# A hybrid attention and RG-LRU block on one Trainium2 core: output-weight passes on GpSimd's DMA queue, a new step order in attention's projection, and another cut of the last rows

## The chip, the cores and the metric

One core of a Trainium2 chip. The metric is the device time of one execution in microseconds. The kernel before took 924.3 us (median of three runs: 921.23, 924.3 and 924.6).

## The reference, cut to what matters

Sequence length and model width are both 1024, everything is float32, and there is one layer.

```python
shift, scale, gate = split(c @ w_ada + b_ada, 3)
h = rmsnorm(x, norm_g) * (1 + scale) + shift
q, k, v, g_attn, xr, g_rnn, m_attn, m_rnn = split(h @ w_in)
y_attn = sliding_window_attention_with_sinks(rope(q), rope(k), v, sinks) * silu(g_attn)
y_rnn = rg_lru(causal_conv4(xr), ...) * silu(g_rnn)
merged = sigmoid(m_attn) * (y_attn @ w_attn_proj) + sigmoid(m_rnn) * (y_rnn @ w_rnn_proj)
x = x + gate * (merged @ w_out)
return rmsnorm(x, final_g)
```

Attention has 16 heads of 64 with 4 key and value heads, blocks of 128 and a window of 128. The three matrix products that the change lies around are `y_rnn @ w_rnn_proj`, `y_attn @ w_attn_proj` and `merged @ w_out`, each 1024 x 1024 x 1024.

## The kernel before, in words

**Precision.** A float32 operand is split into a high part, which ScalarE makes by a cast to fp32r (`cast`, L104, tile `wh` for weights), and a low part, which VectorE makes as the difference (`rest`, L110, tile `wl`). Each product of two operands is three matmuls: high by high, high by low, low by high. So for each half of a weight block (128 x 512) there is a load into a tile `r`, a cast on ScalarE, a subtraction on VectorE, and only then may TensorE use it. Larger products save multiplications in the manner of Strassen: sums and differences of quadrants, seven products in place of eight.

**Order.** Each engine runs its instructions in the order in which the code was written. In the input projection a small planner fills the slots: `run` goes through products of 12 matmuls, a slot of 2.75 us each (`SLOT`, L686), and places background steps from the lists `waiting[0]`, `waiting[1]` and `waiting[2]` where VectorE and ScalarE have room by the planner's own count (`Load.dve`, `Load.act`, `Load.pe`). After the input projection the order is written out by hand. DMAs are issued by SP, and a few by POOL (GpSimd's queue); SP and POOL issue in order, so a DMA whose data isn't there yet holds those behind it in the same queue.

**Stages**, in us of the profiled execution: norm and adaLN to about 113, input projection to about 553, attention's opening to about 620 and the rest of attention to 742, attention's projection to 833, the output product from 833 to the last matmul at about 916.

**Output-weight passes.** `out_weights(kc, cols)` (L1164) prepares `w_out`: eight passes (four row blocks `kc`, two column halves). A pass loads two pieces of `w_out` into the tiles `wq` (`load`, two DMAs of 256 KB), multiplies both by the adaLN gate (`gated`, two VectorE instructions, L1176), and forms sums and differences for the seven products (`one`, `two`, four VectorE instructions of half size, L1181 to L1187). Four stores bring the seven parts to `wq_d` in DRAM. The four tiles are the same for all passes, so a pass's load waits for the stores of the pass before it. The steps stand last in `waiting[2]`, each behind the condition `idle` (L1160); what the input projection doesn't place is left for `outs(n)`, which places `n` steps at a time during attention's projection.

**RNN projection.** It runs as filler inside attention: `rp_steps` yields one `part` per attention unit and calls `load_y` for the next group of `y_rnn` (tiles `yh`, `yl`, from the scratch `yh_d`, `yl_d`, L1441 to L1445).

**Attention's projection** (L1790 to L1840) has eight blocks `c` of 128 output columns, in turn in the PSUM tiles `rp` and `pmain`. After the matmuls of block c are written (`ap_k`), VectorE gets `merge2(c-1)` (projection result times gate, plus the RNN part: two instructions of 128x1024), `naturals(c-1)` (ScalarE cast to `hh`, VectorE rest `hl`: the left operand of the last product), `merge1(c)` (L1726, needs the loads `m`, `smr`), then `prep_r` for the weights of block c+1, then three or four pass steps (`outs`) and for c over 4 the quadrant sums (`sums`). `merge_loads(c+1)` issues the three loads that the merges of block c+1 need.

**The output product** (L1862 on) goes by 24 steps n = 0..23, each 12 x 4 matmuls into four of eight PSUM banks `bo`, and a last round that is done row by row (p = 6). `prep_right(n+4)` splits the weights `wr` four steps ahead. At n = 3 ScalarE copies four banks into the four others (`A.copy(b1[i], b2[i])`, L1929); step n = 4 adds to these copies. From n = 21 on the first half of the final norm's rows is scaled (`row1`, tile `xo`), and the last round ends with `row2` for each of four row blocks: root of the mean square, scale on ScalarE and VectorE, store.

## Time and profile before

| | us |
|---|---|
| median of the runs | 924.3 |
| profiled execution, its own time | 925.58 |
| its span, first instruction to last | 923.9 |
| TensorE busy in the span | 896.8 (97%) |
| VectorE busy | 722.7 (78%) |
| ScalarE busy | 555.7 (60%) |
| GpSimd busy | 90.7 (10%) |

The 1.68 us between the profiled execution's time and its span lie outside the recorded instructions. A row of a timeline gives start, duration, engine, line, operation, output and inputs, the number of merged instructions, and in brackets the idle time ahead of it with what ended that. TensorE's matmuls are pipelined, so a row of one matmul shows 0.39 us although the next starts 0.23 us later.

### The profile page before, as it was taken

The page shows a single profiled execution, that of the slowest core. Times are in us where ns is not written, and L with a number is a line of the kernel's source. Part 1 is how long each engine was busy: PE and PEld are TensorE (multiplying, and loading weights), DVE is VectorE, ACT ScalarE, POOL GpSimd, SP SyncE. Part 2 cuts the span into 40 slices and gives each one's busy share as a digit, 9 for nine tenths or more (in the row PEclk, how much of TensorE's full clock was granted, in tenths as well). Part 3 has the DMA queues.
Part 4 walks back from the last instruction along what each step waited for, and adds up shares of the span by engine and source line. Part 5 has one row for each costly group of instructions (what it writes and reads, how often), then busy time and mean ns, then how long its engine had stood idle before and what let it go on. Part 6 is the DMA issues. An engine that isn't in the chain of part 4 may idle for free.

```text
span 923.9 us, 12581 instructions
## 1 busy us (share of the span) xinstructions
PE 896.8 (97%) x4187; PEld 741.8 (80%) x4187; DVE 722.7 (78%) x1139; ACT 555.7 (60%) x1084; POOL 90.7 (10%) x156
## 2 busy tenths in 40 slices
PE   5999999999999999999999999999999999998996
PEld 4789888887888888888887888888888878776885
DVE  7976889797659975997677776898999738669675
ACT  6753655554557646775596785887878611114554
POOL 0110000000000000000000002544354300000002
PEclk9999999999999999999999999999999999999999
DMA  9943459862342651445145349996665188896214
GB/s 354 414 168 113 166 169 322 276 210 79 115 137 91 205 200 49 148 165 192 57 147 196 102 171 335 350 349 211 196 202 167 57 289 276 306 368 239 66 58 168
DMA packets 97047, 182.06 MB, mean 197 GB/s; under 512 B 13891, under 2 KB 41539, under 8 KB 96982
## 3 DMA queue, kind: packets, MB, share of 16 engines
q1 hardware_dynamic: 93940, 173.11, 54.3%
q0 software_dynamic: 2752, 7.83, 2.4%
q8 instruction: 33, 0.54, 0.2%
q10 hardware_dynamic: 290, 0.32, 0.1%
q14 instruction: 32, 0.26, 0.1%
HBM read 124.49 MB, written 57.12 MB: 197 GB/s over the span
## 4 chain that ended last, share of the span: by engine, by line
PE 74%; DMA 11%; DVE 9%; ACT 3%; issue 2%; SPq 1%; POOL 0%; DVEq 0%; ACTq 0%; POOLq 0%
PE bk L693 43%; PE rp L174 7%; PE bo L1862 5%; PE pgate L988 5%; PE bk L174 3%; PE pv L1350 2%; PE s_ps L1278 2%; DMA wq_d<-wq 2%; PE pmain L174 2%; DMA yl<-yl_d 1%; DMA wq<-w_out 1%; PE pt L1316 1%; DMA r<-w_rp 1%; DVE wl L110 1%; DMA r<-w_main 1%
## 5 line engine op out<-in xcount | busy, mean ns | idle before, releaser
L693 PE MATMUL bk<-nh,wl 128*128 128x512 f32 x352 | 137.6, 391 | 1.4 <-DVE wl L110 1.4
L693 PE MATMUL bk<-nh,wh 128*128 128x512 f32 x352 | 137.3, 390 | 0.0
L693 PE MATMUL bk<-nl,wh 128*128 128x512 f32 x352 | 137.2, 390 | 0.0
L110 DVE TENSOR_TENSOR wl<-r,wh 128x512 fp32r<-128x512 f32 x113 | 80.7, 728 | 19.7 <-ACT wh L104 19.7
L104 ACT CAST wh<-r 128x512 fp32r<-128x512 f32 x113 | 68.6, 618 | 35.2 <-PE bk L1524 12.2
L693 PEld LDWEIGHTS bk<-nh,wl 128*128 128x128 f32 x352 | 66.1, 188 | 16.3 <-DVE wl L110 2.7
L693 PEld LDWEIGHTS bk<-nh,wh 128*128 128x128 f32 x352 | 66.1, 188 | 13.6
L693 PEld LDWEIGHTS bk<-nl,wh 128*128 128x128 f32 x352 | 66.1, 188 | 13.6
L693 PE MATMUL bk<-hh,wh 128*128 128x512 f32 x176 | 68.7, 390 | 0.0
L693 PE MATMUL bk<-hh,wl 128*128 128x512 f32 x176 | 68.6, 390 | 0.0
L693 PE MATMUL bk<-hl,wh 128*128 128x512 f32 x176 | 68.6, 390 | 0.0
L110 DVE TENSOR_TENSOR wl<-ws,wh 128x512 fp32r<-128x512 f32 x76 | 51.7, 684 | 0.5 <-ACT wh L104 0.5
L1302 ACT ACTIVATE p<-p,small 128x129 f32<-128x129 f32 x128 | 50.1, 400 | 0.0
L60 POOL DMA_DIRECT2D yh_d<-yh x1 | 0.6, 557 | 493.8 <-ACT yh L1055 493.8
L104 ACT CAST wh<-ws 128x512 fp32r<-128x512 f32 x76 | 45.8, 613 | 1.2 <-DVE ws L715 1.1
L1862 PE MATMUL bo<-wh,sum 128*128 128x512 f32 x128 | 39.6, 390 | 0.0
L693 PEld LDWEIGHTS bk<-hh,wh 128*128 128x128 f32 x176 | 33.1, 188 | 7.6 <-ACT wh L104 0.9
L693 PEld LDWEIGHTS bk<-hl,wh 128*128 128x128 f32 x176 | 33.1, 188 | 6.9
L693 PEld LDWEIGHTS bk<-hh,wl 128*128 128x128 f32 x176 | 33.1, 188 | 6.7
L1278 PE MATMUL s_ps<-ks,qs 128*128 128x256 f32 (+1 forms) x256 | 37.6, 289 | 0.1
L796 ACT ACTIVATE c<-bk 128x512 f32<-128x512 f32 x29 | 17.3, 597 | 32.8 <-PE bk L693 32.8
L693 PE MATMUL bk<-hha,wl 128*128 128x512 f32 x88 | 34.4, 391 | 0.1
(408 smaller groups left out, 2326.2 us busy)
## 6 DMA issues: line engine op xcount, KB each, us to landing
r<-w_main SPq DMA_DIRECT2D x100, 256.0 KB, 4.3
wada<-w_ss SPq DMA_DIRECT2D x16, 512.5 KB, 8.8
qs<-q_d SPq DMA_DIRECT2D x16, 512.0 KB, 6.6
wq_d<-wq SPq DMA_DIRECT2D x24, 256.0 KB, 6.2
wr<-wq_d SPq DMA_DIRECT2D x24, 256.0 KB, 5.0
ks<-k_d SPq DMA_DIRECT2D x24, 192.0 KB, 4.7
q_d<-rhi SPq DMA_DIRECT2D x16, 256.0 KB, 4.1
q_d<-rlo SPq DMA_DIRECT2D x16, 256.0 KB, 4.2
```

The costliest lines, as they stand in the source:

```text
L60: return eng.dma_start(dst, src)
L104: A.copy(dst[0][:], src)
L110: V.tensor_tensor(out=dst[1][:], in0=src, in1=f32(dst[0][:]), op=ALU.subtract)
L174: mm = T.matmul(ps[hf], ww, xx[kc][hf], start=(kc == 0 and ww is w_h and xx is xh), stop=(kc == KC - 1 and xx is xl))
L693: W["pe"] = T.matmul(ps, ww[:, c], b[kc][xx_], start=(first and kc == 0 and i == 0), stop=(kc == 3 and i == 2), skip_group_check=not first)
L796: A.activation(t["t"], s(), AF.Tanh, scale=0.5)
L988: W["pe"] = T.matmul(ps[:, SL[hf]], ww[:, c0:c0 + P], xx_[:, SL[hf]], start=(ic == 0 and i == 0), stop=(ic == 1 and i == 2))
L1278: W["pe"] = T.matmul(o, qs[:, j, qc], ks[:, b, k0 + (0 if n else P):k0 + 256], start=(b == 0), stop=(b == 1))
L1302: A.activation(px[:, j, :], px[:, j, :], AF.Exp, bias=sm[:, 0, j:j + 1], accum_out=sm[:, 1, j:j + 1])
L1316: W["pe"] = T.transpose(pt[:, j, :], px[:, j, 0:P], ident[:])
L1350: W["pe"] = T.matmul(pv[:], b, m[:].rearrange("p j q -> p (j q)"), start=(i == 0), stop=(i == len(prods) - 1))
L1862: T.matmul(bank[p][i] if dst is None else dst, a[:, ts_], b[:][:, sl], start=(new and kc == 0 and j == 0), stop=(kc == 3 and j == 2), skip ...
```

## The change

Four things change.

1. The six DMAs of an output-weight pass are issued on POOL (argument `G`) in place of SP. The load no longer waits for `idle`. `idle` is false from slot 130 on, and two stretches of slots (`ROOMY`) let a step in although gate steps wait, where the planner's count has VectorE at most 2.8 us ahead of TensorE. With that, three passes and the load of the fourth stand ahead of attention (before: two passes, and the load of the third, whose arithmetic and stores stood at attention's opening). Five passes' arithmetic and four loads are left for attention's projection (before: five and five).
2. `load_y` is called one unit sooner for the last four groups.
3. In attention's projection the weights of block c+1 are prepared ahead of the merges, `merge1(c)` stands ahead of `merge2(c-1)`, `sma` is loaded in a step of its own (`merge_load2`), passes and sums come last, and the first weights of the output product (`load_b11`, `prep_right(0..3)`) and the sums stand one to two blocks away from where they stood. The copies of the PSUM banks stand ahead of `prep_right(7)`. `fg_bc` and all loads of `x1` move to n = 0.
4. Last rows: the first half of `xo` is multiplied by `fg_bc` at n = 9 and 10 (four VectorE instructions of 128x512), so that `row1` scales that half on ScalarE and VectorE does the other half; two rows stand at n = 21 and two at n = 22 (before: one and three). In the last round the matmuls, addition and square of the last row's first cut stand ahead of the root of row 2.

```diff
+    ROOMY = (52, 56), (111, 117)
...
     def idle():
-        return not waiting[0] or waiting[0][0] in asks
+        t = W["slot"]
+        return t < 130 and (not waiting[0] or waiting[0][0] in asks or (
+            any(a <= t < b for a, b in ROOMY) and Load.dve <= Load.pe + 2.8))
...
         def load():
             for t, k in ((t1, kc), (t2, kc + 4)):
                 dma(t[:], w_out[k * P:(k + 1) * P, :].rearrange(
-                    "p (a t) -> p a t", a=2)[:, :, cols])
+                    "p (a t) -> p a t", a=2)[:, :, cols], G)
...
-            dma(wq_d[kc][:, 0, cols], b11)
-            dma(wq_d[kc][:, 3:5, cols], t2[:])
+            dma(wq_d[kc][:, 0, cols], b11, G)
+            dma(wq_d[kc][:, 3:5, cols], t2[:], G)
...
-            dma(wq_d[kc][:, 1:3, cols], t3[:])
+            dma(wq_d[kc][:, 1:3, cols], t3[:], G)
...
-            dma(wq_d[kc][:, 5:7, cols], t4[:])
-
-        return [idle, [("S", 0, 0, load)], slots(2), idle, [("D", 0, 1.38, gated)], idle,
-                [("D", 0, 0.84, one)], idle, [("D", 0, 0.84, two)], slots(2)]
+            dma(wq_d[kc][:, 5:7, cols], t4[:], G)
+
+        return [[("S", 0, 0, load)], slots(2), idle, [("D", 0, 1.38, gated)], idle,
+                [("D", 0, 0.84, one)], idle, [("D", 0, 0.84, two)], slots(1)]
...
         for i, (c, k) in enumerate(seq):
             part(c, k)
-            if i in (1, 2, 3, 4):
-                load_y(i + 3)
+            if i in (0, 1, 2, 3):
+                load_y(i + 4)
...
+
+    def merge_load2(c):
         ss[c] = tpool.tile([P, S], F32, tag="ss", name="sma", bufs=2)
         dma(ss[c][:], sma_d[c])
...
-    merge2(0)
-    naturals(0)
     merge1(1)
     merge_loads(2)
+    merge2(0)
+    merge_load2(2)
+    naturals(0)
     outs(4)
     for c in range(2, KC):
         ps[c] = new_ps()
         ap_k(c, range(KC))
         if c + 2 < KC:
             load_r(KC + c + 2)
-        merge2(c - 1)
-        naturals(c - 1)
+        if c + 1 < KC:
+            for i in range(2):
+                prep_r(KC + c + 1, i)
         merge1(c)
         if c + 1 < KC:
             merge_loads(c + 1)
-            for i in range(2):
-                prep_r(KC + c + 1, i)
-        if c == 4:
-            fg_bc = W["tout"].tile([P, S], F32, tag="rp", name="fg_bc")
-            dma(fg_bc[:], rows[0:1, D:2 * D].to_broadcast([P, D]))
+        merge2(c - 1)
+        if c + 1 < KC:
+            merge_load2(c + 1)
+        naturals(c - 1)
+        if c < 5:
+            outs(4)
+        if c > 5:
+            for n in ((0,), (1, 2, 3))[c - 6]:
+                prep_right(n, first_w[n])
+        if c in (5, 6):
+            sums(c - 5)
         if c == 5:
-            for i in range(2):
-                load_x1(i, "xo", 2)
-        if c == 6:
             load_b11()
-            prep_right(0, first_w[0])
-        if c == 7:
-            for n in (1, 2):
-                prep_right(n, first_w[n])
-        if c < 6:
-            outs(4)
-        if c > 4:
-            sums(c - 5)
-        if c == 7:
-            prep_right(3, first_w[3])
...
     def row1(i):
-        V.scalar_tensor_tensor(out=x1[i][:], in0=x1[i][:], scalar=pcol(0, i), in1=fg_bc[:],
-                               op0=MUL, op1=MUL)
+        a, b = [x1[i][:, t] for t in SL]
+        A.activation(a, a, AF.Copy, scale=pcol(0, i))
+        V.scalar_tensor_tensor(out=b, in0=b, scalar=pcol(0, i), in1=fg_bc[:, SL[1]], op0=MUL,
+                               op1=MUL)
         dma(out[i * P:(i + 1) * P, :], x1[i][:])
...
-    def row2(i, f, eng=nc.sync):
+    def scale2(i, f, eng=nc.sync):
         a, b = x2[i]
-        root(f)
         A.activation(b, b, AF.Copy, scale=f[:, 3:4])
         V.scalar_tensor_tensor(out=a, in0=a, scalar=f[:, 3:4], in1=fg_bc[:, SL[0]], op0=MUL,
                                op1=MUL)
...
         if n == 0:
             naturals(7)
-            for i in range(2):
-                load_x1(2 + i, "ss", 2)
-        if n + 4 < 28:
-            prep_right(n + 4)
-        if n == 2:
-            sums(3)
+            for i in range(4):
+                load_x1(i, "ss" if i > 1 else "xo", 2)
+            fg_bc = W["tout"].tile([P, S], F32, tag="rp", name="fg_bc")
+            dma(fg_bc[:], rows[0:1, D:2 * D].to_broadcast([P, D]))
         if n == 3:
             for i in range(4):
                 A.copy(b1[i], b2[i])
+        if n + 4 < 28:
+            prep_right(n + 4)
+        if n in (2, 4):
+            sums(2 if n == 2 else 3)
...
-        at = {4: ("S1", 0), 5: ("S1", 1), 8: ("NS4", 0), 10: ("NS4", 1), 12: ("S2", 0),
+        at = {5: ("S1", 0), 7: ("S1", 1), 8: ("NS4", 0), 10: ("NS4", 1), 12: ("S2", 0),
               14: ("S2", 1), 16: ("NS3", 0), 18: ("NS3", 1)}
...
+        if n in (9, 10):
+            for i in (2 * n - 18, 2 * n - 17):
+                TT(out=x1[i][:, SL[0]], in0=x1[i][:, SL[0]], in1=fg_bc[:, SL[0]], op=MUL)
         if n == 21:
             roots1()
-            row1(0)
-        if n == 22:
-            for i in range(1, 4):
+        if n in (21, 22):
+            for i in (2 * n - 42, 2 * n - 41):
                 row1(i)
...
+    fs = [small() for _ in range(3)]
+
+    def last_cut(h, f):
+        sl = slice(256 * h, 256 * h + 256)
+        for kc in range(4):
+            products(6, kc, 3, b1[2 + h][:, 0:256], sl, True)
+        add_x(x2[3][0][:, sl], b1[2 + h][:, 0:256], ADD)
+        square(x2[3][0][:, sl], f[:, 1:2] if h else f[:, 4:5], 256)
     for i in range(3):
-        f = small()
+        f = fs[i]
         guard(f, pcol(8, i))
         for kc in range(4):
             products(6, kc, i)
         add_x(x2[i][0], b2[i], ADD)
         square(x2[i][0], f[:, 1:2])
-        row2(i, f)
+        if i < 2:
+            root(f)
+            scale2(i, f)
     f = small()
-    cuts = [slice(0, 256), slice(256, HALF)]
-    for h, sl in enumerate(cuts):
-        for kc in range(4):
-            products(6, kc, 3, b1[2 + h][:, 0:256], sl, True)
-        add_x(x2[3][0][:, sl], b1[2 + h][:, 0:256], ADD)
-        square(x2[3][0][:, sl], f[:, 1:2] if h else f[:, 4:5], 256)
-        if not h:
-            TT(out=f[:, 5:6], in0=f[:, 4:5], in1=pcol(8, 3), op=ADD)
-            guard(f, f[:, 5:6])
-    row2(3, f, A)
+    last_cut(0, f)
+    root(fs[2])
+    TT(out=f[:, 5:6], in0=f[:, 4:5], in1=pcol(8, 3), op=ADD)
+    guard(f, f[:, 5:6])
+    last_cut(1, f)
+    scale2(2, fs[2])
+    root(f)
+    scale2(3, f, A)
```

TensorE's instructions stand in the same order before and after. On other engines the order moves at these places.

SP at attention's opening, before: the load and the four stores of the third pass (`wq`, `wq_d`) stand among the loads for attention (`ks`, `qs`, `sink`).

```order
L60 DMA smr_d_118<-c 128x512
L60 DMA wq_79<-w_out 128x2x256
L60 DMA wq_80<-w_out 128x2x256
L60 DMA ks<-k_d 64x2x256 x2
L60 DMA qs<-q_d_98 128x4x256
L60 DMA sink<-rows 128x16
L60 DMA ks<-k_d 64x2x384 x2
L60 DMA qs<-q_d_98 128x4x256
L60 DMA wq_d_147<-wq_79 128x256
L60 DMA wq_d_147<-wq_80 128x2x256
L60 DMA wq_d_147<-wq_81 128x2x256
L60 DMA wq_d_147<-wq_82 128x2x256
```

SP at the same place, after:

```order
L60 DMA smr_d_118<-c 128x512
L60 DMA ks<-k_d 64x2x256 x2
L60 DMA qs<-q_d_98 128x4x256
L60 DMA sink<-rows 128x16
L60 DMA ks<-k_d 64x2x384 x2
L60 DMA qs<-q_d_98 128x4x256
```

And POOL at that place, after (the two rows of `wq` are the fourth pass's load; before, POOL had the rows from `yh_d` on):

```order
L60 DMA wq_79<-w_out 128x2x256
L60 DMA wq_80<-w_out 128x2x256
L60 DMA yh_d_129<-yh 128x1024
L60 DMA yl_d_137<-yl 128x1024
L1269 COPY p<-sink 128x4
L60 DMA dv<-dv_d_93 128x256
L60 DMA vs<-vs_d_89 128x128
L60 DMA smr_d_118<-c 128x512
L60 DMA smr_d_119<-c 128x512
L1298 AFFINE_SELECT p<-p 128x4x128
```

The pass's load moved from SP to POOL, ahead of the stores of `yh`, and its stores are gone from this place: those of three passes stand earlier on POOL, the others after attention.

VectorE in attention's projection, before: from `merge1(2)` to the end of `naturals(2)`. `wl` are the next block's weights, `wq` a pass, `m`, `sma` and `hla` the merges and naturals.

```order
L1726 SCALAR_TENSOR_TENSOR m<-smr,m 128x1024
L110 TENSOR_TENSOR wl<-r,wh 128x512 x2
L1176 TENSOR_TENSOR wq_79<-wq_79,gate_bc 128x512
L1176 TENSOR_TENSOR wq_80<-wq_80,gate_bc 128x512
L1181 TENSOR_TENSOR wq_81<-wq_79 128x256
L1182 TENSOR_TENSOR wq_81<-wq_79,wq_80 128x256
L1186 TENSOR_TENSOR wq_82<-wq_80,wq_81 128x256
L1187 TENSOR_TENSOR wq_82<-wq_80,wq_82 128x256
L1730 SCALAR_TENSOR_TENSOR sma<-sma,rp_5600 128x1024
L1732 TENSOR_TENSOR m<-m,sma 128x1024
L1739 TENSOR_TENSOR hla_177<-m,hha_175 128x512
```

VectorE up to the end of `naturals(2)`, after:

```order
L1179 TENSOR_TENSOR wq_79<-wq_79,gate_bc 128x512
L1179 TENSOR_TENSOR wq_80<-wq_80,gate_bc 128x512
L1184 TENSOR_TENSOR wq_81<-wq_79 128x256
L1185 TENSOR_TENSOR wq_81<-wq_79,wq_80 128x256
L1189 TENSOR_TENSOR wq_82<-wq_80,wq_81 128x256
L1190 TENSOR_TENSOR wq_82<-wq_80,wq_82 128x256
L110 TENSOR_TENSOR wl<-r,wh 128x512 x2
L1731 SCALAR_TENSOR_TENSOR m<-smr,m 128x1024
L1735 SCALAR_TENSOR_TENSOR sma<-sma,rp_5602 128x1024
L1737 TENSOR_TENSOR m<-m,sma 128x1024
L1744 TENSOR_TENSOR hla_177<-m,hha_175 128x512
```

The pass moved to the start, behind the naturals of block 1, and `wl` and `merge1` stand ahead of `merge2` and the naturals; the `wl` rows here are those of block 4, which before stood only after these rows.

VectorE where attention's projection passes into the output product, before: `merge1(7)` to the first weights of `wr`. The rows `m<-m` are quadrant sums.

```order
L1726 SCALAR_TENSOR_TENSOR m<-smr,m 128x1024
L110 TENSOR_TENSOR wl<-r,wh 128x512 x2
L1745 TENSOR_TENSOR m<-m 128x512
L1746 TENSOR_TENSOR m<-m 128x512
L1747 TENSOR_TENSOR m<-m 128x512
L1748 TENSOR_TENSOR m<-m 128x512
L110 TENSOR_TENSOR wl<-r,wh 128x512
L1730 SCALAR_TENSOR_TENSOR sma<-sma,pmain 128x1024
L1732 TENSOR_TENSOR m<-m,sma 128x1024
L1739 TENSOR_TENSOR hl_190<-m,hh_189 128x512 x2
L110 TENSOR_TENSOR wl<-wr,wh 128x512 x3
```

VectorE from `merge1(7)` on, after:

```order
L1731 SCALAR_TENSOR_TENSOR m<-smr,m 128x1024
L1735 SCALAR_TENSOR_TENSOR sma<-sma,rp_5602 128x1024
L1737 TENSOR_TENSOR m<-m,sma 128x1024
L1744 TENSOR_TENSOR hl_188<-m,hh_187 128x512 x2
L110 TENSOR_TENSOR wl<-r,wh 128x512 x3
L1735 SCALAR_TENSOR_TENSOR sma<-sma,pmain 128x1024
L1737 TENSOR_TENSOR m<-m,sma 128x1024
L1744 TENSOR_TENSOR hl_190<-m,hh_189 128x512 x2
L110 TENSOR_TENSOR wl<-wr,wh 128x512 x3
```

Four rows of sums moved away from between `merge1(7)` and `merge2(7)`, and `merge2(6)` with `naturals(6)` moved in, behind `merge1(7)`; the three `wl` of the output product's first steps stand together ahead of `merge2(7)`.

More of the change, by code (lines that the diff above doesn't have):

```diff
@@ L1791, in tile_hybrid_block @@
     merge_loads(0)
+    merge_load2(0)
     load_r(KC + 3)
@@ L1796, in tile_hybrid_block @@
     merge_loads(1)
+    merge_load2(1)
     ap_k(1, range(6))
```

## Prediction

> **What bounds the kernel now.** I read the profile page's busy times first, then TensorE's share stage by stage (windows), then what TensorE waited for (waits), then the timelines around each wait. The first row is from the page, the others are windows; their columns are stretch, length, busy time of TensorE, weight loads, VectorE, ScalarE, GpSimd, then granted clock, DMA share and GB/s.
>
> ```profile
> PE 896.8 (97%) x4187; PEld 741.8 (80%) x4187; DVE 722.7 (78%) x1139; ACT 555.7 (60%) x1084; POOL 90.7 (10%) x156
> ...
> 113.00:486.00 373.00, 372.90 (x1641) 306.94 (x1640) 297.71 (x434) 235.01 (x348) 0.00 (x0) 1.00 0.47 159
> 553.00:620.00 67.00, 65.84 (x351) 55.69 (x350) 56.26 (x101) 49.70 (x153) 27.47 (x49) 1.00 1.00 345
> 740.00:847.00 107.00, 102.16 (x444) 82.53 (x442) 72.29 (x103) 20.81 (x37) 0.00 (x0) 1.00 0.84 295
> 848.00:851.60 3.60, 3.60 (x11) 2.80 (x10) 3.53 (x6) 2.27 (x5) 0.00 (x0) 0.53 0.95 361
> ```
>
> TensorE is the bound: 896.8 of 923.9 us, and the change takes no matmul away. Only its idle time can be gained, 27.1 us. The input projection (113 to 486) has nothing to give: 372.90 of 373. The second place to look is attention's opening, where the DMA engines are full (share 1.00), the third attention's projection, with 107.00 - 102.16 = 4.84 us idle. Behind that, 3.6 us ran at a granted clock of 0.53. Which waits they are, from the table of TensorE's waits (engine, line, what it waited for: us in total, times, longest):
>
> ```profile
> PE bo L1862 <- ACT bo L1929: 1.9, 1, 1.9
> PE bk L693 <- DVE wl L110: 1.4, 2, 1.0
> PE pmain L174 <- DVE wl L110: 1.1, 1, 1.1
> PE bo L1862 <- DVE xo L1867: 1.1, 1, 1.1
> ...
> PE bo L1862 <- DVE wl L110: 0.9, 1, 0.9
> PE rp L174 <- DVE wl L110: 0.6, 1, 0.6
> PE pmain L174 <- ACT wh L104: 0.6, 1, 0.6
> PE rp L174 <- DMA yl<-yl_d: 0.6, 1, 0.6
> PE rp L174 <- DMA yh<-yh_d: 0.2, 1, 0.2
> ```
>
> The longest waits, for the first x, stand at the start, which the change leaves alone. Each wait costs more than the table says, since the matmuls' overlap has to build up again. TensorE's timeline at the opening shows it:
>
> ```profile
> 566.12 0.39 PE L693 MATMUL bk<-nl,wh 128*128 128x512 f32 x1
> 566.35 1.11 PE L1278 MATMUL s_ps<-ks,qs 128*128 128x256 f32 x8
> 567.30 0.39 PE L693 MATMUL bk<-nh,wh 128*128 128x512 f32 x1
> 568.67 0.51 PE L693 MATMUL bk<-nh,wl 128*128 128x512 f32 x1 [0.98 <-DVE wl L110]
> ```
>
> A matmul of 512 columns starts 566.35 - 566.12 = 0.23 after the one before it; here it was 568.67 - 567.30 = 1.37. So this wait of 0.98 cost 1.14: 0.16 on top, which I add to each wait.
>
> **The change part by part.** *Attention's opening.* The chain of waits runs from SP's issue to the late `wl` (the first two rows below are SP's timeline, the others the chain):
>
> ```profile
> 552.99 1.23 SPq L60 DMA_DIRECT2D wq<-w_out  x2
> 560.00 2.98 SPq L60 DMA_DIRECT2D wq_d<-wq  x4
> ```
>
> ```profile
> 557.12 0.58 SPq L60
> 557.75 6.73 DMA ks<-k_d
> 564.48 0.54 POOL dv L60
> ...
> 568.02 0.61 DVE wl L110
> ```
>
> The load `wq` stood 1.23 us of issue ahead of `ks`, and moved 512 KB at 345 GB/s, 1.5 us of all engines. Both go: up to 2.7 us sooner against a stall of 1.14, so all of **1.14** is gained; the bound below is 0, if `ks` lands late for its neighbours alone. The third pass's VectorE work goes to slots of the input projection, where VectorE has 373 - 298 = 75 us free. A planner's slot can still hold back one subtraction; one pass is 2.7 us of VectorE (below), so I take 0.5 lost, between 0 and 2.7, since the free time is 28 times that.
>
> *y one unit sooner.* The chain has the last `yl` landing right where TensorE resumes:
>
> ```profile
> 612.12 13.08 DMA yl<-yl_d
> 625.24 0.73 PE rp L174 x2
> ```
>
> The last group is issued some 2 us sooner, the one before it by a unit. The waits 0.6 + 0.2 with two build-ups of 0.16 are **1.1**, gained if the landing stays 13.08; at worst 0.
>
> *Attention's projection.* VectorE's timeline:
>
> ```profile
> 767.82 1.29 DVE L1176 TENSOR_TENSOR wq<-wq,gate_bc 128x512 f32<-128x512 f32 x2
> 769.02 0.42 DVE L1181 TENSOR_TENSOR wq<-wq 128x256 f32<-128x256 f32 x1
> ...
> 790.26 0.69 DVE L1176 TENSOR_TENSOR wq<-wq,gate_bc 128x512 f32<-128x512 f32 x1 [2.14 <-DMA wq<-w_out]
> 792.17 0.69 DVE L1176 TENSOR_TENSOR wq<-wq,gate_bc 128x512 f32<-128x512 f32 x1 [1.22 <-DMA wq<-w_out]
> ...
> 799.15 1.29 DVE L110 TENSOR_TENSOR wl<-r,wh 128x512 fp32r<-128x512 f32 x2
> ```
>
> VectorE stands still for a pass's load (2.14 + 1.22 at 790), and the weights `wl` behind it come at 799.15, just too late for TensorE (1.1). With `wl` ahead of the merges that wait goes, and the same at 811 (0.6): 1.26 + 0.76 = **2.0**. SP's queue gives another:
>
> ```profile
> 743.68 3.14 SPq L60 DMA_DIRECT2D wq_d<-wq  x4
> 746.87 1.02 SPq L60 DMA_DIRECT2D r<-w_ap  x2
> ```
>
> The weights `w_ap` stood behind the stores for 3.14 us; with the stores on POOL they are issued at once, and `wh` (0.6) comes in time: **0.8**.
>
> *Into the output product.* ScalarE copies four banks (2.03 us) behind `wh` and the naturals of block 7, and these stood behind four sums and a `wl` on VectorE, from which ScalarE got `m` only at 843.5:
>
> ```profile
> 841.03 1.21 DVE L1730 SCALAR_TENSOR_TENSOR sma<-sma,pmain 128x1024 f32<-128x1024 f32 x1
> 846.66 2.03 ACT L1929 COPY bo<-bo 128x512 f32<-128x512 f32 x4
> ```
>
> In the new order `merge2(7)` can start when TensorE ends block 7, at 833, and the copies stand ahead of `prep_right(7)`, so they start when step 3 has filled the banks. TensorE's 1.9 + 0.16 = **2.1** go; so do the 0.9 + 0.16 = **1.1** for an earlier `wl`. If the low clock follows from the gap, 3.60 x (1 - 0.53) = **1.7** go with it. At worst VectorE, holding four sums at n = 2 and four at n = 4 there, is late again and only half is gained.
>
> *Last rows.* TensorE's 1.1 + 0.16 = **1.3** wait is for an addition behind this:
>
> ```profile
> 899.67 3.67 DVE L1901 SCALAR_TENSOR_TENSOR xo<-xo,pk_t,fg_bc 128x1024 f32<-128x1024 f32 x3
> ```
>
> After the change two instructions of half size stand there in place of three whole ones. With 0.7 each (the `wq` instructions of 128x512), that is 1.4 in place of 3.7, and 2.3 covers 1.3. The four multiplications at n = 9 and 10 lie in VectorE's free time. The end's other order gives about **0.2** on VectorE (a root off the last row's path), between 0 and 0.5.
>
> Sum: 1.1 + 1.1 + 2.0 + 0.8 + 2.1 + 1.1 + 1.7 + 1.3 + 0.2 = 11.4.
>
> *What POOL's queue costs.* The five passes after attention form a chain of their own: a pass's tile is free when its store has landed, and then the next load must land. A cycle is P = 1.3 (two `gated`) + two landings. The view of DMA issues has SP's landings in the projection (median us at the end of the row):
>
> ```profile
> wq_d<-wq SPq DMA_DIRECT2D x15, 256.0 KB, 6.3
> wq<-w_out SPq DMA_DIRECT2D x10, 256.0 KB, 4.2
> ```
>
> The same view has SP's `wq_d` at the opening, and the view of the tile `smr_d` has what POOL's queue took there for seven stores of the same 256 KB:
>
> ```profile
> wq_d<-wq SPq DMA_DIRECT2D x3, 256.0 KB, 8.4
> ```
>
> ```profile
> DMA to landing us min/median/max: 4.4/5.9/7.6
> ```
>
> P is 1.3 + 6.3 + 4.2 = 11.8 as on SP, 13.1 with twice 5.9, 16.5 with twice 7.6. A block is 48 matmuls of 0.23, 11 us. Pass 5 stands at about 767, as before; pass 8, three cycles later, has the weights of block 6 behind it: 767 + 3P + 2.7 of pass + 1.3 of `wl` = 771 + 3P. TensorE needs them at 833 - 2 x 11 = 811, where the table's `rp` waited. Up to P = 13.3 nothing waits; each further us costs 3. I take P = 13.8, twice 5.9 with a little for two loads issued one behind the other: **1.5** lost. Bounds: 0, and 9.6 at P = 16.5. A first `wl` of the output product waiting for late `wq_d` I put at 0.4. So 11.4 - 0.5 - 1.5 - 0.4 = 9.0, and the profiled execution's 925.6 becomes 916.6. It stands 1.3 above the median of 924.3, from which I forecast 924.3 - 9.0 = 915.3.
>
> The Trainium skill ("DMA: Bandwidth & Descriptors", Specifications) gives GpSimd's path a first byte at about 1 us against 0.6 for SP's. By that alone a cycle is an estimated 0.8 longer than with SP's landings, 12.6, which costs nothing, and the time would be 913.8; no row here has the same transfer on both queues at one load.
>
> **The rivals.** *The waits for DMA stay.* At the opening the DMA share is 1.00, so the order of issue may shift who waits and not the sum. For it: 13.08 us for one `yl`. Against: 512 KB leave the crowded stretch. It keeps 1.1 + 1.1: 917.5. The Trainium skill ("Trainium Kernel Development and Optimization", Key Constraints) says that DMAs from SP's, ScalarE's and GpSimd's queues share the same 16 engines and interleave, so that several issuers save issue time only. By that rule the move to POOL alone gains 1.23 of issue at the opening and the 3.14 at 743.68, and no landing gets shorter; the full share of 1.00 agrees.
>
> *The transition keeps its stall.* VectorE is late at 845 all the same, by sums and loads of `x` and `wr` that crowd there; the gap and half clock stay, 2.1 + 1.7: 919.1.
>
> *The passes eat the gain.* POOL's landings are 7 to 8 us each in the projection (share 0.84). P = 15.3 to 17.3 costs 6 to 12, of which 1.5 is in the sum: 919.8 to 925.8. No measurable change.
>
> *Slower.* The same chain, with landings of 9: P = 19.3, pass 8 ends at 771 + 57.9 = 828.9, block 6 waits 17.9, 16.4 more than in the sum: 931.7. It decides from landings of 8.5 on. For it: the 8.4 for `wq_d` at the opening, the 13.08 of `yl`. Against it: the highest of seven POOL landings at share 1.00 was 7.6.
>
> **How the numbers follow.** Forecast as summed, 0.50; DMA waits stay, 0.16; transition stays, 0.10; passes eat it, 0.16; slower, 0.08. A measurement tells this kernel's times apart from about 0.5%, 4.6 us: faster is below 919.7, slower above 928.9. The first three cases lie below 919.7, 0.76 together; 0.02 of it falls to the second and third at once, 915.3 + 2.2 + 3.8 = 921.3. So faster 0.74; same is that 0.02, the fourth case and 0.01 of the fifth, 0.19; slower 0.07. The range begins at 911.0: all gains without residue give 924.3 - 11.4 = 912.9, and VectorE's smaller stalls may give 2 more. It ends at 922.5, in the middle of the fourth case.
>
> **What would show it.** Right: no wait over 0.3 at the first `bk` of attention, none for `yl`, no half clock behind the output product's step 3, additions in the last rows at once. The step on POOL is right if the five `gated` after attention lie 11 to 14 us apart and landings of `wq` are 5 to 6.5. Wrong: TensorE waiting over 3 us for `wl` in blocks 5 or 6 with VectorE idle ahead of `wq` for `w_out`, or a low clock again at 845.

## The result, and the profile after

The changed kernel takes 915.88 us (median of four runs, 915.62 to 917.0), the kernel before 923.79 in the same comparison (four runs, 921.23 to 924.6). The ratio is 0.9921, its 95% interval 0.99 to 0.9943: 7.9 us faster, forecast were 9.0 and a time of 915.3. The profiled execution took 915.79, its span is 914.1, against 925.58 and 923.9 before. So the two traces lie 9.8 us apart, 1.9 more than the medians, because the profiled execution of before lies 1.8 above its own median. Terms below are counted between the traces.

From the page, then windows, of the changed kernel:

```profile
PE 893.5 (98%) x4187; PEld 740.2 (81%) x4187; DVE 722.1 (79%) x1143; ACT 557.7 (61%) x1088; POOL 124.8 (14%) x204
...
113.00:486.00 373.00, 371.99 (x1633) 305.38 (x1632) 299.53 (x439) 233.14 (x347) 12.57 (x18) 1.00 0.48 163
...
553.00:620.00 67.00, 66.80 (x357) 56.73 (x356) 55.11 (x97) 50.49 (x154) 27.59 (x49) 1.00 0.97 330
...
740.00:847.00 107.00, 106.74 (x471) 88.05 (x471) 76.20 (x109) 25.28 (x45) 19.50 (x28) 1.00 0.86 306
847.00:890.00 43.00, 42.08 (x185) 34.21 (x184) 31.82 (x55) 23.55 (x47) 0.00 (x0) 1.00 0.20 69
```

Attention's opening lost 1.16 us of TensorE's time before and loses 0.2 now; attention's projection and the steps behind it lost 4.84 and lose 0.26, at a clock of 1.00 throughout. Two stretches got worse: the input projection loses 1.01 in place of 0.10, and 847 to 890 loses 0.92 (0.29 before). The table of TensorE's waits of the changed kernel:

```profile
PE bk L694 <- DVE wl L110: 1.3, 3, 0.5
...
PE bo L1864 <- DVE xo L1869: 0.9, 2, 0.6
PE bo L1864 <- DVE wl L110: 0.3, 1, 0.3
```

The waits for `yl`, `yh`, for `wl` and `wh` in the projection and for the bank copies are gone. The 0.9 for `xo` are two new ones, at 851 and 863 and not ahead of the last round. The 1.3 for `wl` now are three waits of 0.4 to 0.5: one at 495, as before, and two new ones at 306 and 315.

VectorE's timeline of the changed kernel shows the passes on POOL's queue:

```profile
765.63 1.29 DVE L1179 TENSOR_TENSOR wq<-wq,gate_bc 128x512 f32<-128x512 f32 x2
...
776.81 0.69 DVE L1179 TENSOR_TENSOR wq<-wq,gate_bc 128x512 f32<-128x512 f32 x1 [2.31 <-DMA wq<-w_out]
780.44 0.69 DVE L1179 TENSOR_TENSOR wq<-wq,gate_bc 128x512 f32<-128x512 f32 x1 [2.93 <-DMA wq<-w_out]
...
788.62 1.29 DVE L1179 TENSOR_TENSOR wq<-wq,gate_bc 128x512 f32<-128x512 f32 x2
...
801.83 0.69 DVE L1179 TENSOR_TENSOR wq<-wq,gate_bc 128x512 f32<-128x512 f32 x1 [4.34 <-DMA wq<-w_out]
803.78 0.69 DVE L1179 TENSOR_TENSOR wq<-wq,gate_bc 128x512 f32<-128x512 f32 x1 [1.26 <-DMA wq<-w_out]
...
805.86 1.29 DVE L110 TENSOR_TENSOR wl<-r,wh 128x512 fp32r<-128x512 f32 x2
```

From the second `gated` of pass 5 (766.2) to that of pass 8 (803.78) are three cycles of 12.5 on average, 14.2, 8.8 and 14.6 one by one; 13.8 was forecast. The prediction's sign, 11 to 14 us apart, holds for their mean and for none of the three by itself. The weights of block 6, at 805.86, came in time. So far the prediction holds. Which edit did it is another matter, and the experiments say so.

### The profile page after: what moved, and what is told of

The parts are those of the page before. It is cut to its first block, busy times and chain, and to the rows that moved or that the text cites. A ratio compares the mean times of both kernels' runs of the same rounds, so it can differ in the third digit from the quotient of the medians.

```text
span 914.1 us, 12609 instructions
## 1 busy us (share of the span) xinstructions
PE 893.5 (98%) x4187; PEld 740.2 (81%) x4187; DVE 722.1 (79%) x1143; ACT 557.7 (61%) x1088; POOL 124.8 (14%) x204
## 4 chain that ended last, share of the span: by engine, by line
PE 75%; DVE 9%; DMA 7%; issue 5%; ACT 3%; POOL 1%; SPq 0%; DVEq 0%; ACTq 0%; POOLq 0%
PE bk L694 42%; PE rp L174 7%; PE bo L1864 6%; PE pgate L989 5%; PE bk L174 3%; PE s_ps L1281 3%; PE pv L1353 2%; DMA wq_d<-wq 2%; DVE wl L110 2%; DMA wq<-w_out 2%; PE pt L1319 1%; PE pmain L174 1%; DMA wada<-w_ss 1%; DMA r<-w_main 1%; PE bk L1527 1%
## 5 line engine op out<-in xcount | busy, mean ns | idle before, releaser
L60 POOL DMA_DIRECT2D wq_d<-wq x32 | 21.9, 685 | 424.7 <-DVE wq L1179 379.5
L694 PEld LDWEIGHTS bk<-nh,wh 128*128 128x128 f32 x352 | 66.1, 188 | 13.8
```

The lines of the kernel that those rows point to most:

```text
L60: return eng.dma_start(dst, src)
L694: W["pe"] = T.matmul(ps, ww[:, c], b[kc][xx_], start=(first and kc == 0 and i == 0), stop=(kc == 3 and i == 2), skip_group_check=not first)
```

## The experiments

Each kernel is the changed kernel with the edit shown, unless the text says otherwise. The experiments were timed in three groups, each beside the kernel before: its median was 922.7 for experiments 1, 6, 8 and 9, 923.48 for 3, 4, 5 and 7, and 923.15 for 2, 10 and 11. The changed kernel's own 915.88 comes from a fourth group, so a difference of one or two microseconds from it has to be read from the traces and not from the medians.

**1. The passes on SP's queue, in the new order.**

```diff
-                    "p (a t) -> p a t", a=2)[:, :, cols], G)
+                    "p (a t) -> p a t", a=2)[:, :, cols])
...
-            dma(wq_d[kc][:, 0, cols], b11, G)
+            dma(wq_d[kc][:, 0, cols], b11)
```

(and so in the other stores)

> The changed kernel with the DMAs of all output-weight passes back on SP's queue, in the new order, nothing else undone. Theory (each edit pays its own term, and the queue pays where SP would stand): SP must now wait for each pass's stores before it may issue the next pass's load, about 5 us each time, and the weights w_ap and the merges' loads stand behind it. I expect 2 to 6 us more than the changed kernel, 918 to 922, with TensorE waiting for wl or wh in blocks 3 to 7 of attention's projection. Rival (the 16 DMA engines are the same for every queue, a queue saves issue time only): the issue of the waiting weights moves by 0.8 us, so 0 to 1 us more, and no wait over 1 us in the projection. Landings of wq on SP and on POOL at nearly the same load are compared in the traces: the theory has POOL's longer by at most 1 us.

Measured: 915.3 us (914.97 to 915.62), ratio to before 0.9908 (0.9884 to 0.9933), no slower than the changed kernel. The projection has no wait at all. My theory of the queue fell: SP does stand behind the stores, but nothing that stands with it is late. The view of the tile `wq` from 740 to 850 gives who waited for it, first on POOL (the changed kernel), then on SP (this one):

```profile
  DVE wq L1179: 10.9, 4
```

```profile
  DVE wq L1179: 2.5, 3
```

VectorE waits 10.9 us for the passes on POOL and 2.5 on SP. The view of DMA issues from 742 to 808 splits that by direction, POOL first:

```profile
wq_d<-wq POOLq DMA_DIRECT2D x15, 256.0 KB, 5.5
...
wq<-w_out POOLq DMA_DIRECT2D x8, 256.0 KB, 6.3
```

```profile
wq_d<-wq SPq DMA_DIRECT2D x15, 256.0 KB, 6.1
...
wq<-w_out SPq DMA_DIRECT2D x8, 256.0 KB, 4.1
```

A store and a load take 11.8 on POOL and 10.2 on SP: 1.6 more per cycle, where I had allowed 1. It is the load that is longer. Whether by its queue or because SP, free of the stores, sends its own large loads into the same time, these runs don't separate.

**2. The queue alone, in the kernel before.** The same five arguments `G`, put into the kernel before, with nothing else of the change.

> The kernel before with one part of the change alone: the six DMAs of every pass on POOL's queue. Theory (the queue has no gain of its own, the order made room for it): the wait for w_ap at 750 (0.77) goes, but POOL's loads for attention (dv, vs) stand behind the stores of the opening's pass, and in the projection wl of blocks 4 to 6 come later than before behind longer cycles; 2 to 8 us more than before, 925 to 932, waits of over 2 us for wl or wh in blocks 4 to 6. Rival (SP's queue was what held things up): 1 to 3 us less than before.

Measured: 933.67 us (932.3 to 935.38), ratio 1.0107 (1.0079 to 1.0136): 10.5 us slower, more than I had expected. From the table of waits, and the windows of the opening:

```profile
PE bk L693 <- DVE wl L110: 4.4, 2, 4.0
PE rp L174 <- ACT wh L104: 2.7, 1, 2.7
...
PE rp L174 <- DVE wl L110: 2.5, 2, 1.3
PE bo L1862 <- ACT bo L1929: 1.8, 1, 1.8
```

```profile
553.00:620.00 67.00, 62.51 (x324) 52.50 (x323) 51.80 (x93) 45.36 (x139) 30.18 (x52) 0.97 0.95 323
```

4.0 us go at attention's opening and 5.2 in the projection, each with a stretch at half clock behind it. The first no rival had named, and its cause is not the one that I expected: POOL issues attention's `dv` at 561.78, sooner than in the kernel before (564.48). It is the pass's own load that comes late. POOL issues it at 556.21, behind the stores of `yh` and `yl`, where SP did at 552.99; VectorE stands for it, and the weights `wl` that TensorE needs stand behind the pass:

```profile
564.33 0.69 DVE L1176 TENSOR_TENSOR wq<-wq,gate_bc 128x512 f32<-128x512 f32 x1 [5.39 <-DMA wq<-w_out]
...
566.82 0.69 DVE L110 TENSOR_TENSOR wl<-r,wh 128x512 fp32r<-128x512 f32 x1
```

In the projection it is the prediction's rival of slower passes, brought about by the queue with the old order.

**3. The old order of attention's projection, the passes on POOL.** The calls from `merge_loads(0)` to `load_wr("B21")` as in the kernel before.

```diff
-        if c + 1 < KC:
-            for i in range(2):
-                prep_r(KC + c + 1, i)
+        merge2(c - 1)
+        naturals(c - 1)
         merge1(c)
...
+            for i in range(2):
+                prep_r(KC + c + 1, i)
```

> The changed kernel with attention's projection in the old order (merge2 and naturals ahead of merge1, weights of the next block after the merges, sums, first weights and the loads of x and fg_bc at their old places), the passes still on POOL, the copies and the last rows as changed. Theory (the order is what paid in the projection): waits for wl in blocks 5 and 6, at the first steps of the output product and for the copies come back, together 4 to 7 us with the clock. Rival (the queue paid, since SP no longer stands for the stores): less than 1.5 us of waits from 740 to 847.

Measured: 926.86 us (925.68 to 928.21), ratio 1.0039 (1.002 to 1.0059): slower than the kernel before, 11 us above the changed kernel. From its waits, and a window:

```profile
PE rp L174 <- ACT wh L104: 2.7, 1, 2.7
...
PE rp L174 <- DVE wl L110: 2.0, 2, 1.3
PE bo L1865 <- ACT bo L1929: 1.4, 1, 1.4
```

```profile
788.00:794.80 6.80, 6.03 (x13) 4.30 (x14) 6.73 (x12) 0.52 (x1) 2.74 (x4) 0.50 0.79 227
```

The order pays, and on POOL's queue it is needed. My 4 to 7 us were short, since one wait of 2.84 from start to start at 785 was followed by 6.8 us at half clock. VectorE stands for the pass's load there (the first row; another 2.26 follow for its second piece), `merge2` behind it comes late, and ScalarE, which needs `m`, casts the weights only after that:

```profile
779.32 0.69 DVE L1179 TENSOR_TENSOR wq<-wq,gate_bc 128x512 f32<-128x512 f32 x1 [4.62 <-DMA wq<-w_out]
```

```profile
786.86 0.62 ACT L1740 CAST hha<-m 128x512 fp32r<-128x512 f32 x1 [14.17 <-DVE m L1735]
```

Queue and order make a table of four: old order on POOL 926.9, new order on POOL 915.9, new order on SP 915.3; the fourth, old order on SP, was run only without the other edits, as the kernel before.

**4. The bank copies behind `prep_right(7)`** (one execution).

```diff
-        if n == 3:
-            for i in range(4):
-                A.copy(b1[i], b2[i])
         if n + 4 < 28:
             prep_right(n + 4)
+        if n == 3:
+            for i in range(4):
+                A.copy(b1[i], b2[i])
```

> The changed kernel with ScalarE's four bank copies of step 3 put back behind prep_right(7); nothing else. Theory as predicted (the copies' own place ahead of prep_right(7) was needed): TensorE waits about 1.5 to 2 us for the copies again and the granted clock falls, 3 to 4 us more. Rival (the block-7 merge and naturals, 8 us sooner than before, are what did it): by ScalarE's timeline of the changed kernel a cast of 0.6 us slips ahead of the copies and they still end ahead of their need; no wait, 0 us.

Measured: 916.4 us, span 914.7, no wait for the copies. So their own place did nothing, as far as one execution shows. ScalarE's timeline of the changed kernel shows why, with VectorE's `merge2(7)` ahead of it:

```profile
832.88 1.22 DVE L1735 SCALAR_TENSOR_TENSOR sma<-sma,pmain 128x1024 f32<-128x1024 f32 x1
```

```profile
836.44 1.66 ACT L104 CAST wh<-wr 128x512 fp32r<-128x512 f32 x3
838.04 2.61 ACT L1930 COPY bo<-bo 128x512 f32<-128x512 f32 x4
```

`merge2(7)` starts 8 us sooner than before, and the copies are early enough to wait for their banks.

**5. The bank copies in reverse order**, to make the gap of the kernel before again.

```diff
-            for i in range(4):
+            for i in (3, 2, 1, 0):
                 A.copy(b1[i], b2[i])
```

> The changed kernel with the four bank copies in reverse order, so that TensorE's next step has to wait for the last of them. This makes on purpose a gap like that of the kernel before, about 2 us, at the same place. Theory (the half clock of 3.4 us in the kernel before followed from the gap): the gap of about 2 us is followed by a granted clock of 0.5 for about 3.4 us, and the time rises by 3.5 to 4. Rival (the half clock was a chance of that execution): the gap costs its 2 us and the clock stays at 1.00.

Measured: 920.08 us (918.55 to 922.48), ratio 0.9972 (0.9957 to 0.9987), 4.2 above the changed kernel; the spans are 3.7 apart. TensorE's timeline, then the window behind the gap:

```profile
839.41 0.39 PE L1864 MATMUL bo<-wh,hla 128*128 128x512 f32 x1
841.93 0.60 PE L1864 MATMUL bo<-wh,hh 128*128 128x512 f32 x1 [2.13 <-ACT bo L1930]
```

```profile
842.20:845.60 3.40, 3.40 (x9) 2.62 (x9) 3.10 (x5) 0.72 (x2) 0.00 (x0) 0.50 1.05 410
```

The gap takes 2.52 - 0.23 = 2.29 and the half clock 3.4 x 0.5 = 1.7. So the half clock does follow from the gap, and the wait is worth nearly twice what the table of waits says of it. That need not be so in every execution: the mean granted clock was 0.996 in six of the ten and 0.997 or 0.998 in four.

**6. y at its old places.**

```diff
-            if i in (0, 1, 2, 3):
-                load_y(i + 4)
+            if i in (1, 2, 3, 4):
+                load_y(i + 3)
```

> The changed kernel with load_y called at its old places. Theory: it was the later issue of y that made TensorE wait; the waits for yl and yh come back with 0.5 to 1 us in all, and the time rises by 1.1 us at most, which only the trace can tell. Rival: the pass that left attention's opening took its traffic away, and y would have come in time without an earlier issue; no wait for y, 0 us.

Measured: 917.51 us (916.33 to 918.58), ratio 0.9932 (0.9906 to 0.9958). There is no wait for `y` in the trace: the rival is right. The profiled execution has another wait, in block 6 of the projection:

```profile
PE rp L174 <- DVE wl L110: 1.5, 1, 1.5
```

That is the wait which the prediction put at 1.5 for the passes on POOL. In the seven profiled kernels with the new order and POOL it was absent four times and came to 1.5, 1.1 and 0.4 in the others, never in the three on SP. It does not need this edit, since it came at 1.1 and 0.4 with `y` issued sooner (experiments 11 and 8); the 1.6 us between the medians are not shown to be the cost of the edit.

**7. The third pass at attention's opening**, planned as before, on SP's queue; all else as changed.

```diff
-        t = W["slot"]
-        return t < 130 and (not waiting[0] or waiting[0][0] in asks or (
-            any(a <= t < b for a, b in ROOMY) and Load.dve <= Load.pe + 2.8))
+        return not waiting[0] or waiting[0][0] in asks
```

(and the list of a pass's steps as before)

> The changed kernel with the old planning of the passes (two before attention, the third at attention's opening) on SP's queue; y, the projection's order and the last rows as changed. Theory: the third pass at the opening is what held the loads of attention up; the wait for wl at the first bk of attention (1 us) comes back, and with it 1.1 us. As y stays sooner, the waits for y tell whether an early y alone would have been enough: none by the prediction. The two waits of the planner's other order at 306 and 315 (0.57 and 0.66) go. In sum -0.5 to +0.5 us against the same kernel without the pass at the opening (915.3). Rival: the opening's wait came from the other loads, and stays away.

Measured: 915.96 us (915.11 to 918.39), ratio 0.9927 (0.9902 to 0.9952); the span is 914.5 against 913.3 in experiment 1. From the waits:

```profile
PE s_ps L1280 <- DMA qs<-q_d: 1.8, 1, 1.8
```

The opening's wait comes back with the pass, but at another load: `qs`, at 564, and 1.8. No wait for `y`. The two waits at 306 and 315 are gone. They had cost 0.57 and 0.66 from start to start, 1.23 together. As the span is 1.2 longer without them, the pass at the opening costs about 2.4 in this order, of which the wait for `qs` is 1.99 from start to start.

**8. `row1` as before.** The old `row1` (one instruction of 128x1024 on VectorE), one row at n = 21 and three at n = 22, no multiplications at n = 9 and 10.

```diff
-        A.activation(a, a, AF.Copy, scale=pcol(0, i))
...
-            for i in (2 * n - 42, 2 * n - 41):
+            for i in ((0,), (1, 2, 3))[n - 21]:
```

> The changed kernel with row1 as before: one VectorE instruction of 128x1024 a row, one row at n = 21 and three at n = 22, and no multiplications at n = 9 and 10. Theory: the wait for xo of about 1.1 us ahead of the last round comes back, 1.3 us more; the wait at 862 (0.3 us), which has the multiplications of n = 9 and 10 ahead of its addition, goes, 0.5 us less. Rival: the earlier merges left VectorE enough room at the end, the wait stays away; 0.5 us less in all.

Measured: 917.38 us (916.34 to 918.11), ratio 0.993 (0.9905 to 0.9955). The wait is back, and the one at 863 is gone:

```profile
PE bo L1864 <- DVE xo L1869: 1.7, 2, 1.1
```

1.1 of it stands ahead of the last round, as before the change; the other 0.6 is the one at 851.

**9. The last round as before.** Root and scaling of row 2 ahead of the last row's first cut.

```diff
-    last_cut(0, f)
-    root(fs[2])
...
-    last_cut(1, f)
-    scale2(2, fs[2])
+    for h, sl in enumerate(cuts):
```

> The changed kernel with the old order of the last round (the root of row 2 and its scaling ahead of the last row's first cut). From the last matmul to the end the changed kernel takes about 7.1 us by its trace and the kernel before 7.9. Theory: this comes from the order, since the last addition no longer stands behind row 2's scaling on VectorE; it goes back to 7.9, 0.8 us more. Rival, as predicted: 0.2 us, the rest being the clock or the landing of the last store; 7.3.

Measured: 917.66 us (916.35 to 919.02), ratio 0.9937 (0.9917 to 0.9958). What counts is the distance from the last matmul to the issue of the last store. TensorE's last matmul and ScalarE's last row in the changed kernel:

```profile
906.69 0.28 PE L1864 MATMUL bo<-wh,hl 128*128 128x256 f32 x1
```

```profile
909.99 0.36 ACTq L60 DMA_DIRECT2D out<-r  x1
```

And in this kernel:

```profile
906.52 0.28 PE L1864 MATMUL bo<-wh,hl 128*128 128x256 f32 x1
```

```profile
910.71 0.37 ACTq L60 DMA_DIRECT2D out<-r  x1
```

3.30 and 4.19: 0.9 us, as the trace had it, and not the 0.2 of the prediction.

**10. A version meant to beat both, on SP.** The passes on SP as in experiment 1, and less work for VectorE ahead of the two additions that TensorE waits for.

```diff
-        at = {5: ("S1", 0), 7: ("S1", 1), 8: ("NS4", 0), 10: ("NS4", 1), 12: ("S2", 0),
+        at = {5: ("S1", 0), 8: ("S1", 1), 9: ("NS4", 0), 10: ("NS4", 1), 12: ("S2", 0),
...
-        if n in (9, 10):
-            for i in (2 * n - 18, 2 * n - 17):
+        if n in (13, 15):
+            for i in (n - 13, n - 12):
```

> A version meant to beat both kernels: the changed kernel with the passes on SP's queue, the second half of the sum S1 at step 8 of the output product (behind the additions of step 7; NS4's first half at step 9), and the four multiplications by fg_bc at steps 13 and 15. Theory (VectorE is behind at steps 7 and 11 because of these instructions, and TensorE waits for its additions): the waits for xo at about 850 and 862 (0.77 and 0.5 us) go, 1.2 us less than with the passes on SP alone, a span of about 912.1 and 914.1 us. Rival: VectorE has so much behind it there that other additions or wl come late in their place; no gain.

Measured: 913.34 us (six runs, 913.24 to 914.52), ratio to before 0.9889 (0.9867 to 0.991). Both waits for `xo` are gone, and 740 to 890 has no idle time left:

```profile
740.00:847.00 107.00, 107.00 (x474) 88.65 (x473) 77.65 (x112) 26.43 (x45) 0.00 (x0) 1.00 0.89 315
847.00:890.00 43.00, 43.00 (x191) 35.61 (x191) 32.66 (x56) 24.42 (x49) 0.00 (x0) 1.00 0.16 56
```

All its runs are below all runs of the changed kernel (915.62 and up), though not taken side by side.

**11. The same version on POOL.** Experiment 10 with the five arguments `G`.

> The same version with the passes on POOL's queue, as changed. It differs from the other one in the queue alone. Theory (after three traces without and two with a wait for wl in block 6 on POOL): 0 to 2 us more than on SP, because a pass's cycle on POOL leaves VectorE waiting for wq about 10 us in all against 2.5 on SP. Rival (the queue is worth something by itself): POOL's version is the faster one by 0.5 us or more.

Measured: 915.76 us (six runs, 914.26 to 916.23), ratio 0.9909 (0.9884 to 0.9933), 2.4 above the version on SP, beside which it was run. Its trace has the block-6 wait and one at the output product's second step:

```profile
PE rp L174 <- DVE wl L110: 1.1, 1, 1.1
...
PE bo L1864 <- DVE wl L110: 0.4, 1, 0.4
```

Neither is in the trace of experiment 10. The queue, which the change is named for, gains nothing in the new order: it costs 2.4 us in this pair, and 0.6 between experiment 1 and the changed kernel, which were not run side by side and lie too close to tell apart.

## Why the prediction was right, and where its steps were not

**Opening, 1.1 forecast.** Right in size, and the pass is the cause: without it the wait is gone, with it (experiment 7) a wait of 1.8 comes. It comes at `qs`, though, and not at the `wl` of the prediction's chain.

**y, 1.1.** The wait went, but not by the step that I gave. Without the pass the old places of `load_y` do as well (experiment 6), and with the pass the new ones do (experiment 7). Either edit alone is enough; the sum counted a gain for the edit that the other had already made.

**wl ahead of the merges, 2.0, and the transition, 2.1 + 1.1.** Right: these waits are gone, and come back with the old order (experiment 3). For the copies I named two reasons, and only the first holds, the early `merge2(7)` (experiment 4).

**The half clock, 1.7.** Right for the profiled execution, and shown (experiment 5). But not every execution of the kernel before has it. Of the 38 that were timed beside the experiments, 18 have a mean granted clock of 0.996 or less, like the profiled one, and a median of 924.7; 20 have 0.997 or more and a median of 922.3. Half a clock lost for 3.4 us of 924 makes 0.002 of the mean, so the second kind had most likely none. The prediction took the 1.7 in full from a median that holds both kinds; this fits the 9.8 between the traces against 7.9 between the medians, but no trace of the second kind was kept.

**w_ap on SP's queue, 0.8.** The step "the weights `w_ap` stood behind the stores for 3.14 us; with the stores on POOL they are issued at once" is true of the kernel before: in experiment 2, where the queue alone moved, SP issues `w_ap` at 742.53 with no store ahead of it, and the wait for `wh` is gone. It failed as the reason in the changed kernel: with the stores on SP in the new order there is no such wait either. SP's timeline of experiment 1:

```profile
741.81 2.42 SPq L60 DMA_DIRECT2D wq_d<-wq  x4
744.28 1.19 SPq L60 DMA_DIRECT2D r<-w_ap  x2
```

The stores still stand ahead, but `w_ap` is issued at 744.28 in place of 746.87. The pass's load was issued long before, at 456.79 in place of 739.47, so the stores start 1.9 us sooner and `w_ap` 2.6 us sooner; TensorE doesn't wait. Either edit alone is enough, as with `y`.

**Last rows, 1.3.** Right (experiment 8).

**The end, 0.2.** Mis-sized: 0.8 to 0.9 (experiment 9), beyond the bound of 0.5. The last addition no longer queues behind row 2's scaling; I had counted only the root.

**POOL's cycle, 1.5 lost.** The mechanism was right, and the size is a matter of the execution: 12.5 per cycle and no wait in the trace of the changed kernel, up to 1.5 of waiting in others of the same order, each time for the `wl` behind pass 8, as foreseen. The rival of slower passes was real, and the order kept it away; with the old order it came (experiments 2 and 3). The Trainium skill's rule ("Trainium Kernel Development and Optimization", Key Constraints), that several issuers save issue time only, agrees with experiments 1 and 11 as far as a gain goes. That the move costs up to 2.4 us in the new order and 10.5 in the kernel before has to be read from the runs.

**Early passes, 0.5 lost.** Mis-sized, 1.23, and by another mechanism than a subtraction held back. The planner, once it has a pass at 262, orders other steps anew; ScalarE's table load and `av`, `rz` stand 7 us later, and VectorE waits for `rz` with `wl` behind it. This is the wait at 306; how the one at 315 arises was not followed up, but both are gone with the old planning (experiment 7):

```profile
301.36 1.28 ACT L1028 ACT_TABLE_LOAD   x1
302.66 1.06 ACT L1028 ACTIVATE av<-rz 128x1024 f32<-128x1024 f32 x1
303.75 1.06 ACT L1031 ACTIVATE rz<-av 128x1024 f32<-128x1024 f32 x1
```

```profile
304.84 1.23 DVE L1034 SCALAR_TENSOR_TENSOR th<-rz,th 128x1024 f32<-128x1024 f32 x1 [1.88 <-ACT rz L1031]
305.99 0.68 DVE L110 TENSOR_TENSOR wl<-r,wh 128x512 fp32r<-128x512 f32 x1
```

**The multiplications at n = 9 and 10 "in VectorE's free time".** This step failed: VectorE is behind there. With S1's second half at step 7 it makes the two new waits, 0.77 and 0.47 from start to start. Experiment 10 moved both and the waits went.

Together: 11.4 were forecast as gains, 12.0 with the end at 0.8 in place of 0.2, and between the traces all of it came. Lost were 1.23, 0.42 at the output product's first steps (0.4 forecast) and 1.24, 2.9 in place of 2.4. That leaves 9.1 of the 9.8 between the traces; the remaining 0.7 is in gaps too small to name. That the total came so close is in part luck. Of the 2.4 forecast as lost, the 1.5 for POOL's cycle did not come in this trace; 1.24 from a step that the prediction put at nothing and 0.73 more from the early passes took its place, and 0.6 more at the end made up for the 0.5 that these cost beyond the forecast. Two edits that weren't needed were counted with gains that others had made already.

## What to carry to other kernels

When several edits aim at the same wait, undo them one at a time before believing any: here the queue that gave the change its name costs up to 2.4 us, and the new order of the steps gave most of what was gained (2.0 + 2.1 + 1.1 + 1.7 = 6.9 of the 12.0 above). In front of an engine that works in order, ask of each instruction which consumer is waiting for those behind it, and put what is needed next (weights) ahead of what is needed later (merges, sums). A wait of two microseconds on TensorE is to be priced with the low clock that can follow it, 1.7 here, though not every execution pays it.

## What the runs showed of the hardware

The half clock follows idle time, but the length of a gap alone does not decide. Gaps beyond the regular pitch of 2.02 (kernel before), 2.29 (experiment 5), 2.84 (experiment 3), and 4.21 and 2.85 (experiment 2) were followed by a clock of 0.50, for 3.4 us, and for 6.8 after the 2.84 and the 2.85, which had a second gap behind them; gaps of 1.70 (experiment 6), 1.99 (experiment 7) and 2.00 (experiment 2, at 853) were not. The row of that last one's window, 1.00 in the clock column:

```profile
853.00:857.00 4.00, 2.16 (x10) 1.48 (x9) 3.93 (x8) 4.00 (x9) 0.00 (x0) 1.00 0.81 264
```

What separates 2.00 from 2.02 shows in when the clock changes. In these traces it falls and rises only at whole multiples of 3.413 us after its first rise: the first fall comes 829.44 us after that in the kernel before (243 times), 826.03 in experiment 5 (242) and 549.55 in experiment 2 (161). If time is cut into these stretches, each gap that was followed by the half clock had 2.02 to 3.23 us of idle time within one stretch (the 2.85 together with its second gap). The gaps of 1.99 and 2.00 lay across the end of a stretch, with at most 1.49 us on one side, and the 1.70 had 1.68 within one. So the edge lies between 1.68 and 2.02 us of idle time within a stretch, by these eight gaps. By this the same gap would bring the half clock in one execution and not in another, which is what the mean clocks of the kernel before suggest.

A load of 256 KB took a median of 6.3 us from POOL's queue and 4.1 from SP's in the same stage, while the stores took 5.5 and 6.1 (experiment 1).
